# Hybrid mixer and expert layer on one core: weight casts and differences chained in the order of use, and none of the differences on POOL

## The chip, the cores and the metric

The kernel runs on one core of a Trainium2 chip. The core has five engines with queues of their own: PE (TensorE, matrix products), DVE (VectorE), ACT (ScalarE), POOL (GpSimd) and SP (SyncE, which here only issues loads). The metric is the device time of one execution in microseconds. The figure of the kernel before is the median of three runs.

## What is computed

One layer over 2048 tokens of width 1024. A layer norm comes first, then a mixer (a gated short convolution and a pooling branch between two projections) with a residual and a second layer norm. The second half is what the change touches: a hierarchical mixture of experts, a gated embedding of p beside it, and the last layer norm.

```python
mix = _hybrid_mixer(x, w_in[i], b_in[i], conv_w[i], pool_w[i], pool_scale[i], w_o[i])
x = _layernorm(DEEPNORM_ALPHA * x + mix, ln1_g[i], ln1_b[i])
ffn = _hierarchical_moe(x, w_router_group[i], b_router_group[i], w_router_expert[i],
                        b_router_expert[i], w1[i], w3[i], w2[i])
ple = jax.nn.sigmoid(x @ w_ple_gate[i] + b_ple_gate[i]) * (p[i] @ w_ple_proj[i])
x = _layernorm(DEEPNORM_ALPHA * x + ffn + ple, ln2_g[i], ln2_b[i])
```

Each token goes to one group of experts and there to two experts, `silu(x @ w1) * (x @ w3) @ w2`. Everything is float32.

## The kernel before

**Products.** A float32 product is made of three matmuls of parts: `mm3` (L222 to L224) multiplies high by high, high by low and low by high. Each operand is split first. `split` (L355 to L357) makes the high part with a cast on ACT (L356) and the low part with a difference on DVE (L357), or on the engine given to it.

**Weights.** The second half uses 414 weight tiles of 128 x 1024 in a fixed sequence. A name such as P0.8 is the weight of kind P, round 0, index 8. Kind P are the ten tiles of the embedding's gate (0 to 3 and 5 to 8) and projection (4 and 9); kinds A and B are the experts'. Rounds P0 and P1 come first, then the experts, then P99 at the end. `load_weights` issues a load on SP (L1132) into a raw slot (RB or RY), `split_weights` (L1137) takes raw tiles in the sequence of use, claims two slots of FB for the parts, issues the cast and the difference, and frees the raw slot. A slot of FB comes free when PE has used its weight. Index 4 and 9 are halved on the way (L1147 on ACT, L1148 on DVE). Of P0 and P1 the odd indexes 1, 3, 5 and 7 have their difference on POOL, eight in all.

**The embedding.** `embed` works on a group of token tiles (10 and 11 with P0, 12 to 15 with P1), the first half of the columns with weights 0 to 4 and the second with 5 to 9. For each tile four gate weights give a PSUM bank; L1280 on DVE adds the bias and frees the bank, L1286 multiplies by the product of p with the projection, L1290 adds the tile's residual, and a store L1321 on POOL writes the finished tile to `based` and frees its raw slot. The tiles of p come in pairs: `fetch_p` (L1188) loads a pair on SP into a raw slot, and `load_p` transposes it on PE (L1221, four transposes) and splits it. L1193 on SP loads the tokens themselves.

**Order.** The instructions are written by jobs that take turns. A scheduler then places them on each engine by a model of times, within the data dependences. An engine works its queue in that order: an instruction that waits holds up all behind it. PE does the router's products (L883, L884), the embedding of P0 and P1, the routing's sums (L1006 to L1026, L1094) and then, behind the barrier of a loop for overflow blocks that here runs no turn (L1707), the experts (first products L1574). Where the loop begins, the engines wait for what was issued before it, stores too.

Of the kernel before, what the change touches and what calls it, by code (L numbers as in the profile page):

```python
# [13 lines left out]
OP = mybir.AluOpType  # L14
# [60 lines left out]
PRE, END = ([10, 11], [12, 13, 14, 15]), [0, 1, 2, 3, 4, 5, 6, 7, 8, 9]  # L75
# [108 lines left out]
def hybrid_conv_pool_hmoe_encoder(ctx, tc, x, p, ln0_g, ln0_b, w_in, b_in, conv_w, pool_w, pool_scale,  # L184
                                  w_o, ln1_g, ln1_b, w_rg, b_rg, w_re, b_re, w1, w3, w2, w_pg, b_pg,
                                  w_pp, ln2_g, ln2_b, out):
    nc = tc.nc
# [3 lines left out]
    FB, RB = Parts(), Parts()  # L191
# [54 lines left out]
    for g in range(4):  # L246
        w = 2 << g
        l, r = w // 2, w // 2 - 1
# [104 lines left out]
        nc.vector.scalar_tensor_tensor(v, v, rstd[:, s:s + 1], b, op0=OP.mult, op1=OP.add)  # L353

    def split(hi, lo, src, eng=nc.vector):  # L355
        nc.scalar.copy(hi, src)  # L356
        eng.tensor_sub(lo, src, hi)  # L357

    def transpose8(src):
        b = SP.get(2, 2)  # L360
# [179 lines left out]
    def load_w(s, j):  # L540

        for i in range(4):
            if (s, j, i) in wz:
                continue
            if (s, j, i) not in raw:
                yield from wait(SR)
                fetch_w(s, j, i)
                yield
            yield from wait(SF)
            hi = SF.get()  # L550
            yield from wait(SF)
            lo = SF.get()
            r = raw.pop((s, j, i))
            split(FB[:, hi], FB[:, lo], RB[:, r])
            SR.free(r)
            wz[s, j, i] = (hi, lo)
            yield
# [128 lines left out]
    def load_wo():  # L686
# [13 lines left out]
        for g in range(4):  # L700
            c = slice(g * 128, (g + 1) * 128)
            nc.scalar.activation(RB[:, r, c], PS[:, b, c], AF.Copy, scale=colsT[:, 28 + g:29 + g])
        SP.free(b)
        split(FB[:, ph, :512], FB[:, pl, :512], RB[:, r, :512])
        SR.free(r)
        yield
# [211 lines left out]
    before = RB[:, L, 896:960].bitcast(BF)  # L918
# [216 lines left out]
                yield  # L1135

    def split_weights():  # L1137
        while True:
            while not raws:
                yield  # L1140
            while sum(i < SF.limit for i in SF.age) < 2 + claims[0]:
                yield
            kind, r, i, q = raws.popleft()
            hi, lo = SF.get(), SF.get()
            if kind == "P" and i % 5 == 4:

                nc.scalar.mul(FB[:, hi], RB[:, q], 0.5)  # L1147
                nc.vector.scalar_tensor_tensor(FB[:, lo], RB[:, q], 0.5, FB[:, hi], op0=OP.mult, op1=OP.subtract)  # L1148
            else:
                split(FB[:, hi], FB[:, lo], RB[:, q], nc.gpsimd if kind == "P" and r < len(PRE) and i % 2 else nc.vector)  # L1150
            SR.free(q)
            wt[kind, r, i] = (hi, lo)
            yield
# [180 lines left out]
    for ts in groups:  # L1334
# [9 lines left out]
        c, q = divmod(ts[-1], 4)  # L1344
# [362 lines left out]
    with tc.For_i(0, nov_n, 1) as it:  # L1707
# [6 lines left out]
        for q in range(2 * NT):  # L1714
            i, t = divmod(q, NT)
# [76 lines left out]
    def pin(ins):  # L1792

        if pinned:
            tc.add_manual_dep(ins.ins, pinned[-1].ins.name,
                              mybir.DependencyInfo(mybir.DependencyClass.NoSync, mybir.DependencyReason.DATA),
                              reason="in order")
        pinned.append(ins)
# [144 lines left out]
    order = [f for fs in plans[:-1] for f in fs] + [END[-1]] + plans[-1]  # L1943
# [40 lines left out]
```

## Time and profile before

| what | value |
|---|---|
| median of three runs | 1607.77 us (1607.4 to 1608.76) |
| the profiled execution | 1608.11 us |
| its span, first to last instruction | 1606.5 us |
| PE busy | 1549.6 us (96%) |
| DVE busy | 1169.4 us (73%) |
| ACT busy | 761.2 us (47%) |
| POOL busy | 456.0 us (28%) |
| mean granted clock of PE | 0.989 |

Durations in the prediction come from the profiled execution, whose time includes 1.6 us around the span. A timeline row gives an instruction's start, its length and, in brackets, how long its engine had stood idle before it and what ended that. Lengths of neighbours overlap by a little, since an engine begins one instruction before the last has drained.

### The profile page before, as it was taken

Reading aid. Unit: us, or ns where it says so; the run is one execution under the profiler, and the core shown is the slowest. Engines: PE = TensorE matmul, PEld = TensorE weight load, DVE = VectorE, ACT = ScalarE, POOL = GpSimd, SP = SyncE. Lnnn points to the kernel's source line nnn. Section 1 sums busy time; section 2 is a strip of 40 time slices with the busy share of each in tenths; the row PEclk is TensorE's granted clock in tenths of the full one; section 3 lists DMA queues with packets and bytes.
Section 4 is the critical chain, followed back from the end, with each engine's and each line's share of the span. In section 5 each row is a group of like instructions: output and inputs, shape, how many; then the busy total and the mean of one; then the engine's idle time right before and its main releaser. Section 6 shows DMA issues by size and latency. Waiting matters only on the chain.

```text
span 1606.5 us, 22561 instructions
## 1 busy us (share of the span) xinstructions
PE 1549.6 (96%) x7836; PEld 1308.6 (81%) x7837; DVE 1169.4 (73%) x1533; ACT 761.2 (47%) x1005; POOL 456.0 (28%) x629
## 2 busy tenths in 40 slices
PE   7999999999999998989999999999999999999893
PEld 7888878887888887778898998888888788878673
DVE  8968574245566768768878888888878876757986
ACT  6242332113111124047777777777777766652220
POOL 3537762441223225010313122111111111013521
PEclk9999999999999999999999999999999999999997
DMA  7546268986376537369698988999999887988961
GB/s 232 194 151 199 68 207 300 352 301 176 117 257 205 175 120 269 117 228 401 247 396 320 406 328 327 395 351 337 353 356 347 318 301 287 371 324 274 339 222 53
DMA packets 205613, 430.64 MB, mean 268 GB/s; under 512 B 19128, under 2 KB 70888, under 8 KB 205496
## 3 DMA queue, kind: packets, MB, share of 16 engines
q1 hardware_dynamic: 161952, 292.06, 50.8%
q0 software_dynamic: 35024, 125.65, 21.5%
q10 hardware_dynamic: 8520, 11.45, 2.0%
q8 instruction: 63, 1.03, 0.3%
q14 instruction: 54, 0.44, 0.1%
HBM read 331.95 MB, written 97.16 MB: 267 GB/s over the span
## 4 chain that ended last, share of the span: by engine, by line
PE 51%; DVE 2%; DMA 1%; issue 0%; ACT 0%; SPq 0%; POOLq 0%; POOL 0%; DVEq 0%; ACTq 0%
PE PS L222 12%; PE PS L224 12%; PE PS L223 12%; PE PS L1574 10%; PE PS L363 2%; PE PS L1520 1%; PE PS L1521 1%; PE PS L1644 1%; DMA RY<-in_p_dram 1%; DMA FB<-x1Td 0%; PE PS L1438 0%; DVE RB L1825 0%; DVE RY L1849 0%; DMA based<-RY 0%; PE PS L1221 0%
## 5 line engine op out<-in xcount | busy, mean ns | idle before, releaser
L223 PE MATMUL PS<-FB 128*128 128x512 f32 (+1 forms) x1364 | 526.0, 386 | 5.9 <-DVE FB L357 5.2
L222 PE MATMUL PS<-FB 128*128 128x512 f32 (+1 forms) x1284 | 496.5, 389 | 17.4 <-DVE ZB L1862 10.1
L224 PE MATMUL PS<-FB 128*128 128x512 f32 (+1 forms) x1284 | 493.6, 386 | 1.6 <-DMA FB<-x1Td 1.1
L357 DVE TENSOR_TENSOR FB<-RY,FB 128x1024 fp32r<-128x1024 f32 x243 | 292.3, 1228 | 51.6 <-ACT FB L356 35.1
L223 PEld LDWEIGHTS PS<-FB 128*128 128x128 f32 x1364 | 258.2, 189 | 56.1 <-DVE FB L357 6.2
L222 PEld LDWEIGHTS PS<-FB 128*128 128x128 f32 x1284 | 242.7, 189 | 66.2 <-DVE ZB L1862 10.3
L224 PEld LDWEIGHTS PS<-FB 128*128 128x128 f32 x1284 | 242.6, 189 | 50.8 <-DMA FB<-x1Td 1.6
L356 ACT CAST FB<-RY 128x1024 fp32r<-128x1024 f32 x247 | 252.6, 1051 | 55.7 <-PE PS L223 18.9
L357 DVE TENSOR_TENSOR FB<-RB,FB 128x1024 fp32r<-128x1024 f32 x197 | 238.5, 1226 | 48.4 <-ACT FB L356 35.1
L356 ACT CAST FB<-RB 128x1024 fp32r<-128x1024 f32 x201 | 207.4, 1052 | 119.6 <-PE PS L223 54.0
L1574 PE MATMUL PS<-FB 128*128 128x296 f32 (+15 forms) x1280 | 174.7, 296 | 3.9 <-issue 3.1
L1574 PEld LDWEIGHTS PS<-FB 128*128 128x128 f32 x1280 | 170.6, 191 | 5.3 <-issue 3.3
L356 ACT CAST FB<-PS 128x1024 fp32r<-128x1024 f32 (+9 forms) x142 | 81.7, 591 | 141.7 <-PE PS L363 83.3
L357 DVE TENSOR_TENSOR FB<-PS,FB 128x1024 fp32r<-128x1024 f32 (+9 forms) x142 | 96.0, 690 | 70.0 <-ACT FB L356 69.6
L1387 POOL DMA_INDIRECT RY<-x1d,TBI x22 | 56.9, 2587 | 172.4 <-DVE FB L357 115.4
L223 PE MATMUL PS<-FB,FY 128*128 128x512 f32 x264 | 104.1, 394 | 0.0
L222 PE MATMUL PS<-FB,FY 128*128 128x512 f32 x216 | 85.7, 397 | 0.0
L224 PE MATMUL PS<-FB,FY 128*128 128x512 f32 x216 | 85.4, 395 | 0.0
L356 ACT CAST FY<-RB 128x1024 fp32r<-128x1024 f32 (+1 forms) x30 | 31.0, 1035 | 109.0 <-PE PS L223 59.5
L1687 POOL DMA_DIRECT2D yd<-RY x25 | 14.3, 573 | 228.5 <-ACT RY L1686 215.6
L1387 POOL DMA_INDIRECT RB<-x1d,TBI x18 | 37.3, 2073 | 144.8 <-DVE FB L357 74.9
L222 PE MATMUL PS<-FY,FB 128*128 128x512 f32 x180 | 71.6, 398 | 0.0
(293 smaller groups left out, 2061.0 us busy)
## 6 DMA issues: line engine op xcount, KB each, us to landing
RY<-in_w_dram SPq DMA_DIRECT2D x233, 512.0 KB, 8.6
RB<-in_w_dram SPq DMA_DIRECT2D x151, 512.0 KB, 9.0
yd<-RB POOLq DMA_DIRECT2D x67, 512.0 KB, 8.0
RB<-in_w_in_dram SPq DMA_DIRECT2D x32, 512.0 KB, 5.7
yd<-RY POOLq DMA_DIRECT2D x25, 512.0 KB, 7.3
RB<-in_x_dram SPq DMA_DIRECT2D x24, 512.0 KB, 4.3
x1Td<-FB POOLq DMA_DIRECT2D x20, 512.0 KB, 6.0
FB<-x1Td SPq DMA_DIRECT2D x20, 512.0 KB, 6.4
```

The costliest lines, as they stand in the source:

```text
L222: nc.tensor.matmul(o, ah, bh, start=start, stop=False)
L223: nc.tensor.matmul(o, ah, bl, start=False, stop=False)
L224: nc.tensor.matmul(o, al, bh, start=False, stop=stop)
L356: nc.scalar.copy(hi, src)
L357: eng.tensor_sub(lo, src, hi)
L363: nc.tensor.transpose(v[:, k], src[:, k * 128:(k + 1) * 128], ident)
L1387: nc.gpsimd.indirect_dma_start(out=RB[0:half or 128, rows[n]], out_offset=None, in_=x1d, in_offset=bass.IndirectOffsetOnAxis(ap=idx, axis=0))
L1520: nc.tensor.matmul(o, xs[0][:, c], wh, start=start, stop=False)
L1521: nc.tensor.matmul(o, xs[0][:, c], wl, start=False, stop=stop)
L1574: nc.tensor.matmul(o, u, v, start=k == 0 and q == 0, stop=k == KD - 1 and q == 1)
L1644: nc.tensor.transpose(v[:, k], g[:, k * 128:(k + 1) * 128], ident[0:m, 0:m])
L1687: nc.gpsimd.dma_start(dst(n), RB[:, q])
```

## The change

`split` returns its two instructions. `split_weights` hands each weight's cast and difference to `pin`, which adds an order-only dependence on the previous one of the same engine in the same block of code. So ACT casts the weights in the sequence of use, and DVE makes the differences in it. The chain starts anew behind the loop. The eight differences that went to POOL go to DVE.

```diff
--- before.py
+++ after.py
@@ -353,8 +353,7 @@
         nc.vector.scalar_tensor_tensor(v, v, rstd[:, s:s + 1], b, op0=OP.mult, op1=OP.add)
 
     def split(hi, lo, src, eng=nc.vector):
-        nc.scalar.copy(hi, src)
-        eng.tensor_sub(lo, src, hi)
+        return nc.scalar.copy(hi, src), eng.tensor_sub(lo, src, hi)
 
     def transpose8(src):
         b = SP.get(2, 2)
@@ -1135,6 +1134,18 @@
                 yield
 
     def split_weights():
+
+        before = {}
+
+        def pin(*made):
+            for made_now in made:
+                ins = made_now.ins
+                if ins.engine in before and before[ins.engine][0] is nc.cur_bb:
+                    tc.add_manual_dep(ins, before[ins.engine][1].name,
+                                      mybir.DependencyInfo(mybir.DependencyClass.NoSync, mybir.DependencyReason.DATA),
+                                      reason="in order")
+                before[ins.engine] = nc.cur_bb, ins
+
         while True:
             while not raws:
                 yield
@@ -1144,10 +1155,10 @@
             hi, lo = SF.get(), SF.get()
             if kind == "P" and i % 5 == 4:
 
-                nc.scalar.mul(FB[:, hi], RB[:, q], 0.5)
-                nc.vector.scalar_tensor_tensor(FB[:, lo], RB[:, q], 0.5, FB[:, hi], op0=OP.mult, op1=OP.subtract)
+                pin(nc.scalar.mul(FB[:, hi], RB[:, q], 0.5),
+                    nc.vector.scalar_tensor_tensor(FB[:, lo], RB[:, q], 0.5, FB[:, hi], op0=OP.mult, op1=OP.subtract))
             else:
-                split(FB[:, hi], FB[:, lo], RB[:, q], nc.gpsimd if kind == "P" and r < len(PRE) and i % 2 else nc.vector)
+                pin(*split(FB[:, hi], FB[:, lo], RB[:, q]))
             SR.free(q)
             wt[kind, r, i] = (hi, lo)
             yield
```

The scheduler then places everything anew. In the kernel before, the casts and differences stood out of sequence in some twenty places on ACT and as many on DVE, most of them around P0, P1 and the first expert; now in none. Lines up to about L1130 have moved by -1 and lines behind by +11: L357 is now L356, L1148 is L1159, L1188 is L1199, L1221 is L1232, L1280 is L1291, L1286 is L1297, L1290 is L1301, L1321 is L1332.

DVE, from the difference of P0.8 on. Before, P0.8 (the first row), P0.9 (L1148), P1.2 and, behind the small routing steps, P1.4 (L1148):

```order
L357 TENSOR_TENSOR FB<-RY,FB 128x1024
L891 TENSOR_TENSOR ZB<-ZB,PS 36x512
L1148 SCALAR_TENSOR_TENSOR FB<-RY,FB 128x1024
L1280 TENSOR_TENSOR ZB<-PS,RB 128x512
L357 TENSOR_TENSOR FB<-RY,FB 128x1024
L1280 TENSOR_TENSOR ZB<-PS,RB 128x512
L967 TENSOR_REDUCE RB<-RB 128x4
L1286 SCALAR_TENSOR_TENSOR ZB<-ZB,PS 128x512
L968 TENSOR_TENSOR RB<-RB 128x16
L945 TENSOR_TENSOR RB<-RB 128x16
L1290 SCALAR_TENSOR_TENSOR RY<-RY,ZB 128x512
L946 TENSOR_TENSOR RB<-RB,down 128x16
```

Now, from the third row behind P0.8, which L1159 of P0.9 precedes as before: P1.0, P1.1, P1.2, P1.3 and P1.4 (L1159), with the first L1301 behind them:

```order
L356 TENSOR_TENSOR FB<-RY,FB 128x1024
L1291 TENSOR_TENSOR ZB<-PS,RB 128x512
L356 TENSOR_TENSOR FB<-RY,FB 128x1024
L1291 TENSOR_TENSOR ZB<-PS,RB 128x512
L356 TENSOR_TENSOR FB<-RY,FB 128x1024
L966 TENSOR_REDUCE RB<-RB 128x4
L1297 SCALAR_TENSOR_TENSOR ZB<-ZB,PS 128x512
L356 TENSOR_TENSOR FB<-RY,FB 128x1024
L1159 SCALAR_TENSOR_TENSOR FB<-RY,FB 128x1024
L967 TENSOR_TENSOR RB<-RB 128x16
L944 TENSOR_TENSOR RB<-RB 128x16
L1301 SCALAR_TENSOR_TENSOR RY<-RY,ZB 128x512
```

The differences of P1.0 and of P1.6, which stood ahead of P0.8, and those of P1.1 and P1.3, which POOL made, have moved in between.

PE, at the transposes of the RY tile of p. Before, they stood behind the routing sums of L1026:

```order
L1026 LDWEIGHTS RB
L1026 MATMUL PS<-OH,RB 128x32
L1221 MATMUL PS<-ident,RB 128x128 x4
L1221 MATMUL PS<-ident,RY 128x128 x4
L1019 LDWEIGHTS RB
L1019 MATMUL PS<-ZB,RB 128x64
L222 MATMUL PS<-FB 128x512
```

Now they stand ahead of P1.5, which is tile 12's second half, behind its last matmul with P1.3:

```order
L222 MATMUL PS<-FB 128x512
L223 MATMUL PS<-FB 128x512
L224 MATMUL PS<-FB 128x512
L1232 MATMUL PS<-ident,RY 128x128 x4
L222 MATMUL PS<-FB 128x512
```

The transposes of the RB tile follow 24 rows later, with the L1006 of the routing.

SP, at the loads of p. Before:

```order
L1193 DMA RY<-x1d 128x1024 x3
L1188 DMA RB<-in_p_dram 128x2x256
L1188 DMA RY<-in_p_dram 128x2x256
L1193 DMA RY<-x1d 128x1024
L1130 TENSOR_LOAD EOR
```

Now:

```order
L1204 DMA RY<-x1d 128x1024 x3
L1199 DMA RY<-in_p_dram 128x2x256
L1199 DMA RB<-in_p_dram 128x2x256
L1204 DMA RY<-x1d 128x1024
L1129 TENSOR_LOAD EOR
```

The two loads of p have changed places.

At the loop, POOL issues three of the last four stores ahead of it instead of four and the fourth behind it, one L1290 of DVE stands behind it too, and the first sixteen L1574 of PE, which stood ahead of the loop, now stand behind it with the rest.

## Rows read from the trace of the kernel before

**Rows 1.** Page, part 1: busy time, share of span, instructions of each engine.
```profile
PE 1549.6 (96%) x7836; PEld 1308.6 (81%) x7837; DVE 1169.4 (73%) x1533; ACT 761.2 (47%) x1005; POOL 456.0 (28%) x629
```

**Rows 2.** Busy time by stretch: stretch, length, five engines, PEclk, DMA share, GB/s.
```profile
645.20:648.60 3.40, 3.40 (x10) 2.63 (x9) 0.87 (x7) 0.00 (x0) 0.00 (x0) 0.50 0.66 242
1527.60:1532.60 5.00, 5.00 (x14) 4.12 (x15) 3.20 (x5) 1.69 (x3) 2.21 (x3) 0.50 0.93 342
```

**Rows 3.** Waits of PE, 590 to 760: engine line, releaser, total, times, longest.
```profile
PE PS L1574 <- issue: 3.1, 1, 3.1
PE PS L223 <- DVE FB L357: 2.9, 1, 2.9
PE PS L222 <- DVE ZB L1280: 2.9, 1, 2.9
PE PS L222 <- DVE FB L357: 1.3, 1, 1.3
```

**Rows 4.** Timeline of PE, 625 to 655: start, length, instruction, [idle before, releaser].
```profile
626.40 0.39 PE L884 MATMUL PS<-FB 128*128 128x512 f32 x1
629.73 0.50 PE L223 MATMUL PS<-FB 128*128 128x512 f32 x1 [2.94 <-DVE FB L357]
...
640.67 0.39 PE L224 MATMUL PS<-FB 128*128 128x512 f32 x1
643.94 0.50 PE L222 MATMUL PS<-FB 128*128 128x512 f32 x1 [2.88 <-DVE ZB L1280]
...
652.23 0.60 PE L1221 MATMUL PS<-ident,RY 128*128 128x128 f32 x4
```

**Rows 5.** Timeline of DVE, 624 to 650.
```profile
626.60 3.07 DVE L357 TENSOR_TENSOR FB<-RY,FB 128x1024 fp32r<-128x1024 f32 x1 [0.23 <-PE PS L883]
...
632.33 1.23 DVE L357 TENSOR_TENSOR FB<-RY,FB 128x1024 fp32r<-128x1024 f32 x1
633.48 0.68 DVE L1280 TENSOR_TENSOR ZB<-PS,RB 128x512 f32<-128x512 f32 x1
...
635.86 2.90 DVE L1290 SCALAR_TENSOR_TENSOR RY<-RY,ZB 128x512 f32<-128x512 f32 x1
...
640.66 0.68 DVE L1290 SCALAR_TENSOR_TENSOR RY<-RY,ZB 128x512 f32<-128x512 f32 x1
...
643.21 0.68 DVE L1280 TENSOR_TENSOR ZB<-PS,RB 128x512 f32<-128x512 f32 x1
```

**Rows 6.** Timeline of POOL, 610 to 720.
```profile
625.25 3.34 POOL L357 TENSOR_TENSOR FB<-RY,FB 128x1024 fp32r<-128x1024 f32 x1
...
635.77 2.45 POOL L357 TENSOR_TENSOR FB<-RY,FB 128x1024 fp32r<-128x1024 f32 x1
639.06 0.57 POOL L1321 DMA_DIRECT2D based<-RY  x1 [0.85 <-DVE RB L946]
...
709.73 0.53 POOL L1321 DMA_DIRECT2D based<-RY  x1 [0.84 <-DVE RY L1290]
```

**Rows 7.** Timeline of SP, 630 to 660: issues of loads.
```profile
641.94 0.38 SPq L1188 DMA_DIRECT2D RB<-in_p_dram  x1
643.99 0.38 SPq L1188 DMA_DIRECT2D RY<-in_p_dram  x1
```

**Rows 8.** DMA issues, whole run: times, KB each, median us from issue to landing.
```profile
RY<-in_p_dram SPq DMA_DIRECT2D x5, 256.0 KB, 6.1
...
RB<-in_p_dram SPq DMA_DIRECT2D x3, 256.0 KB, 3.9
```

**Rows 9.** Timeline of PE, 1522 to 1537.
```profile
1527.54 1.08 PE L1221 MATMUL PS<-ident,RY 128*128 128x128 f32 x4 [4.76 <-DMA RY<-in_p_dram]
```

**Rows 10.** Chain that ended last, 700 to 725.
```profile
712.30 3.33 DMA based<-RY
715.63 1.33 issue
```

**Rows 11.** Timeline of PE, 704 to 730.
```profile
711.33 2.55 PE L1574 MATMUL PS<-FB 128*128 128x384 f32 x16 [0.78 <-DVE ZB L1286]
```

## The prediction

> **What bounds the kernel now.** I read the page's busy times first: PE works 1549.6 of the 1606.5 us [rows 1], so a weight's cast or difference counts only where PE stands waiting for it. The waits of PE around the first two weight rounds come next [rows 3]. There are four that matter: 2.9 us for a low part on DVE, 2.9 us for L1280 on DVE, 1.3 us for another low part and 3.1 us before the first matmuls behind the loop. They are what this change can win between 590 and 760 us, where nearly all the moved instructions are. Last come the timelines of the engines in that stretch.
>
> The first wait is at 629.73: PE's last router matmul starts at 626.40 and the next weight, P0.8, is missing its low part [rows 4]. Its slot is freed by that router work, DVE starts the difference at 626.60 and needs 3.07 us, where the same form takes 1.23 us at 632.33 [rows 5]; POOL's own difference runs from 625.25 for 3.34 us beside it [rows 6]. The second is at 643.94: PE's last matmul before it starts at 640.67, lasts 0.39 us, and tile 12's second half needs the bank that L1280 frees [rows 4], which DVE reaches only at 643.21 [rows 5]. Here, too, POOL held DVE up: L1290, half as wide as a weight, takes 2.90 us at 635.86 [rows 5] beside POOL's difference from 635.77 for 2.45 us [rows 6].
>
> **Part 1: eight differences leave POOL for DVE.** A moved one costs DVE about 1.15 us, the step from 632.33 to 633.48 when it runs back to back [rows 5]. What DVE gets back is the contention: 3.07 - 1.23 = 1.84 us at 626.60 and 2.90 - 0.68 = 2.22 us at 635.86, taking 0.68 us, the length of L1280 at 633.48, as what a 512-wide operation takes [rows 5]. Six of the moved or delayed differences fall between 627 and 645 us and cost 6 x 1.15 = 6.9 us against 4.1 us won, so DVE is later by 2.8 us at the end of the stretch, less what it idled. The first wait shrinks for certain: with POOL silent, the low part of P0.8 takes 1.23 us from 626.60, and PE restarts at 627.9 instead of 629.73, 1.85 us earlier.
>
> The Trainium skill (SBUF — State Buffer, section "Who interferes with whom") says that a DVE instruction with two SBUF inputs and a GpSimd instruction that reads SBUF shut each other out for the whole instruction. By that rule DVE would lose all of POOL's time, the move would be a gain on DVE, and the sum would be that of the faster rival below. The trace shows such blocks in two rows and elsewhere DVE idling while POOL works, so I keep the 4.1 us.
>
> **Part 2: the chain moves DVE's queue.** After P0.8's low part DVE now does, in this order: L891, the low parts of P0.9 and P1.0, L1280, P1.1, L1280, P1.2, L1286, P1.3, P1.4, L1290 and three small steps. That is 6 x 1.15 + 5 x 0.68 + some 0.3 = 10.6 us, so L1290 ends at 627.8 + 10.6 = 638.4. Before, it ended at 635.86 + 2.90 = 638.76 [rows 5]: the added work and the removed contention nearly cancel here. Behind it stand three more low parts (3.45), one L1286 and one L1290 (1.36), the small steps that took 1.9 us from the end of L1290 at 641.34 to 643.21 [rows 5], and L1280 itself (0.68); so L1280 of tile 12 ends at about 645.8 instead of 643.89.
>
> **Part 3: PE's order puts four transposes of p in front of that wait.** This decides my forecast. In the changed order the L1221 transposes of the RY tile of p stand ahead of P1.5, where PE waited at 643.94. Before, they ran at 652.23 [rows 4], long after their data. Their load is bound to a chain: L1290 ends, POOL stores the finished tile (issue 639.06 [rows 6], 0.3 us after L1290), the store lands and frees the slot, and SP issues the load in the same moment, at 643.99 [rows 7]; that is 4.93 us from store to load. SP has the two loads of p swapped, so the RB one (641.94, [rows 7]) no longer goes first, which does not bring the RY one forward: it waits for the store, and the RB one now waits behind it. Now: L1290 638.4, store 638.7, load 643.6. A load of p takes 3.9 us (median of three into RB) to 6.1 us (median of five into RY) from issue to landing [rows 8]. I take 3.8, near the shorter, since this stretch has little other traffic and the longer median holds loads from the crowded end; the bounds are 3.3, which a store twice its size took behind 712.30 [rows 10], and 6.1. PE is ready at 641.06 - 1.85 = 639.2 and stands until 647.4: 8.2 us instead of 2.88. P1.5 starts after the transposes (0.5 us) at 647.9, 4.0 us later than before, and the transposes are missing later on, so the net is **+3.5 us** (bounds +3.0 and +5.8). L1280, done at 645.8, is hidden behind it.
>
> That such a wait happens in this kernel is seen near the end: the same L1221 stood 4.76 us for the same load at 1527.54 [rows 9].
>
> **Part 4: the clock.** After the wait at 643.94 the granted clock was half for the 3.4 us from 645.2, after the longer one at 1527.54 for 5.0 us [rows 2]. Half the clock for a stretch loses half of it: 1.7 us before. After an 8.2 us wait I take the longer stretch, 2.5 us: **+0.8** (0 to +1.7, the latter for twice the shorter stretch). The Trainium skill (TensorE: Matmul & The Clock Gate, section "What's actually happening") has the clock fall to half when the array idles and return after sustained work; the trace agrees with 0.50 behind both waits, and by that rule too a longer wait costs more than its own length.
>
> **Part 5: the loop.** Ahead of the loop POOL now makes three of the four stores of the last tiles instead of four; the fourth, and the sixteen L1574 matmuls that PE did at 711.33 in 2.55 us [rows 11], stand behind it. Before, the last store was issued at 712.30, landed 3.33 us later and PE went on 1.33 us after that [rows 10]. The third was issued at 709.73, 2.6 us earlier [rows 6]. So PE could go on up to 2.6 us earlier, but carries 2.55 us more work behind the loop: between 0 and +2.55. I take 1.0 of the 2.6, since the last products of P1.9 now run in one group: **+1.6**.
>
> **Part 6: the rest.** Of the 414 weights only some twenty changed places on each engine, most of them here. Further on their casts wait for slots that PE frees, and PE does not wait for them: 0 (-1 to +1). With PE held to 647, DVE gets ahead, so the wait of 1.3 us for a low part [rows 3] should halve: **-0.7** (-1.3 to 0). The casts on ACT change places only.
>
> **Sum.** +3.5 + 0.8 + 1.6 - 0.7 = +5.2 us. The first wait's 1.85 us are in the 3.5. The profiled run took 1608.11 us (its span 1606.5 and 1.6 around it), 0.34 above the median of the three runs, so 1613.3 on its scale and **1613.0 us** on the median's. A measurement of this kernel tells about 0.2% (3.2 us) from no change: faster is under 1604.6, slower over 1611.0.
>
> **Rivals.**
> 1. *PE does not wait for p* (no change). If the load is in by 645.3, L1280 decides: P1.5 at 645.8, +1.9; with +1.6 at the loop and -0.7 this gives +2.8, or 1610.6. For it: the load's two medians lie 2.2 us apart. Against: store and load together took 4.9 and at least 3.3 us, so they end at 646.9 from 638.7.
> 2. *POOL's block was the whole cost* (faster). If DVE wins more than 4.1 us from a silent POOL, L1290 and its store come earlier by as much, and the waits at 629.73 and 643.94 and the half clock go: -1.85 - 2.9 - 1.7 + 1.6 = -4.9, or 1602.9. It decides only if both L1280 and p are there by 639.2, 6.6 us and 8.2 us sooner than worked out. For it speaks that POOL held up both of the instructions that PE waited for or stood behind; against it, that DVE has six more weights to do in that time.
> 3. *The fourth store starves the weights* (much slower). It holds a raw slot across the loop, and SP loads in order: the load into that slot waits for it, and those behind too. Issue behind the loop plus a landing of 3.3 us [rows 10] puts some loads 4 us later, +9 in all, 1617. Against: the weights behind have casts much later.
> 4. *The chain does nothing that PE feels*: 1607.8.
>
> **How the numbers follow.** Forecast 0.43, rival 1 0.25, rival 2 0.12, rival 3 0.10, rival 4 0.10. Slower: 0.43 + 0.10 = 0.53; same: 0.35; faster: 0.12. The range from 1606.0 to 1617.0 takes in rivals 1 and 4 and the bounds of part 3, and leaves out rival 2 and half of rival 3.
>
> **What would show it.** PE's wait for a low part at 629.7 down to about 1 us; a wait of L1221 for RY<-in_p of 6 to 9 us near 640; half clock behind it for 3 to 5 us; no L357 on POOL; 96 matmuls of L1574 in one run behind the loop. I am wrong if L1221 finds its data there, if PE's idle time between 620 and 660 falls below 5.8 us, or if a new wait comes up among the experts, where PE is busy throughout.

## Result and profile after: slower, by more than the range allowed

The changed kernel takes 1620.2 us (median of four runs, 1616.87 to 1622.95), the kernel before 1607.68 beside it (1607.4 to 1608.76): 1.0072 times as long, 95% interval 1.0057 to 1.0088. Run once more beside other kernels (e12 below) it stood at 1.0053 (1.0034 to 1.0073). The sign was forecast; the predicted 1613.0 was 7 us short, and the range ended at 1617.0.

The profiled execution of after took 1622.95 us, its span 1621.3. Part 1 of its page answers [rows 1]:

```profile
PE 1559.7 (96%) x7837; PEld 1319.3 (81%) x7837; DVE 1171.3 (72%) x1541; ACT 759.6 (47%) x1005; POOL 442.6 (27%) x621
```

POOL has given up 13.4 us, DVE has only 1.9 more, and PE is *busy* 10.1 us longer on the same matmuls. The same work at a lower clock takes longer, and PE's mean granted clock is 0.979 here, where it was 0.989 before. The waits of PE between 590 and 760 us answer [rows 3] (engine, line, releaser: total, times, longest):

```profile
PE PS L1232 <- issue: 8.0, 1, 8.0
PE PS L1585 <- issue: 6.5, 1, 6.5
PE PS L1585 <- ACT ZB L1293: 1.2, 1, 1.2
PE PS L223 <- DVE FB L356: 1.1, 1, 1.1
PE PS L222 <- DVE ZB L1036: 0.8, 1, 0.8
```

The wait for L1280 (now L1291) is gone; the transposes of p wait instead, and the loop's wait has doubled. The timelines of after answer [rows 4 to 7] (start, length, instruction, idle before it):

```profile
629.33 0.50 PE L223 MATMUL PS<-FB 128*128 128x512 f32 x1 [1.09 <-DVE FB L356]
640.01 0.53 POOL L1332 DMA_DIRECT2D based<-RY  x1 [28.67 <-DVE RY L1301]
645.45 0.68 DVE L1291 TENSOR_TENSOR ZB<-PS,RB 128x512 f32<-128x512 f32 x1
645.86 0.38 SPq L1199 DMA_DIRECT2D RY<-in_p_dram  x1
648.63 1.09 PE L1232 MATMUL PS<-ident,RY 128*128 128x128 f32 x4 [7.95 <-issue]
...
688.70 10.73 PE L1093 MATMUL PS<-RB,RY 128*128 128x40 f32 x64
699.92 0.80 PE L222 MATMUL PS<-FB 128*128 128x512 f32 x1 [0.49 <-DVE TBH L1099]
...
708.15 1.07 PE L222 MATMUL PS<-FB 128*128 128x512 f32 x4
...
732.17 5.05 PE L1585 MATMUL PS<-FB 128*128 128x384 f32 x20 [6.51 <-issue]
```

This execution was 1.45 us later than before's already at the router, from half clock in the first 40 us; the next execution of the same program (e12) was 0.24 us later there. The chain of work that ended last, at the loop, answers [rows 10]:

```profile
726.03 4.62 DMA based<-RY
730.66 1.51 issue
732.17 7.90 PE PS L1585 x40
```

The prediction does not speak of L1093, the small matmuls of 40 columns that put the token numbers into blocks by masks which DVE makes (L1088). They are 32 instructions of the program and 64 in the trace. Before they ran in two halves of 32:

```profile
674.01 3.66 PE L1094 MATMUL PS<-RB,RY 128*128 128x40 f32 x32
677.50 0.47 PE L222 MATMUL PS<-FB 128*128 128x512 f32 x1
...
681.72 3.66 PE L1094 MATMUL PS<-RB,RY 128*128 128x40 f32 x32
...
694.86 1.07 PE L222 MATMUL PS<-FB 128*128 128x512 f32 x4
```

A half took 3.49 us to the next matmul's start, with 18 products of 0.227 us between the halves. In after all 64 stand in one run and take 10.73 us instead of twice 3.49. The windows of after through that run say why (stretch, length, PE, PEld, DVE, ACT, POOL, PEclk, DMA share, GB/s):

```profile
690.00:691.00 1.00, 1.00 (x12) 1.00 (x11) 0.39 (x1) 0.00 (x0) 0.00 (x0) 1.00 0.00 0
692.00:693.00 1.00, 1.00 (x7) 1.00 (x7) 0.36 (x1) 0.00 (x0) 0.00 (x0) 0.50 0.00 0
696.00:697.00 1.00, 1.00 (x7) 1.00 (x6) 0.00 (x0) 0.00 (x0) 0.00 (x0) 0.50 0.00 0
704.00:705.00 1.00, 1.00 (x4) 0.82 (x3) 0.99 (x1) 0.00 (x0) 0.08 (x1) 0.50 1.06 410
706.00:707.00 1.00, 1.00 (x6) 0.80 (x5) 0.41 (x1) 0.56 (x1) 0.00 (x0) 1.00 1.02 410
```

PE is busy for the whole of each of these microseconds, and yet its clock falls to 0.50 (1.2 instead of 2.4 GHz) near 692 and is back only near 705.6, among the products behind. Before, the clock was 1.00 through the same work, from the first small matmul to the first product of P1.8 (window of before):

```profile
674.00:694.80 20.80, 20.80 (x125) 18.39 (x124) 10.65 (x14) 6.46 (x7) 2.94 (x3) 1.00 0.55 198
```

### The profile page after: what moved, and what is told of

Same layout as the page of the kernel before. It is cut to its first block, busy times and chain, and to the rows that moved or that the text cites. A ratio compares the mean times of both kernels' runs of the same rounds, so it can differ in the third digit from the quotient of the medians.

```text
span 1621.3 us, 22544 instructions
## 1 busy us (share of the span) xinstructions
PE 1559.7 (96%) x7837; PEld 1319.3 (81%) x7837; DVE 1171.3 (72%) x1541; ACT 759.6 (47%) x1005; POOL 442.6 (27%) x621
## 4 chain that ended last, share of the span: by engine, by line
PE 89%; DVE 5%; issue 2%; POOL 2%; DMA 1%; ACT 1%; POOLq 0%; DVEq 0%; ACTq 0%
PE PS L222 23%; PE PS L224 23%; PE PS L223 23%; PE PS L1585 10%; PE PS L362 3%; PE PS L1531 1%; PE PS L1532 1%; DVE FB L356 1%; PE PS L1093 1%; PE PS L1655 1%; DVE RY L1836 1%; DVE RB L1836 0%; DVE RY L1860 0%; PE PS L882 0%; PE PS L883 0%
## 5 line engine op out<-in xcount | busy, mean ns | idle before, releaser
L356 DVE TENSOR_TENSOR FB<-RY,FB 128x1024 fp32r<-128x1024 f32 x247 | 294.6, 1218 | 53.5 <-ACT FB L356 35.2
L356 ACT CAST FB<-RY 128x1024 fp32r<-128x1024 f32 x247 | 251.7, 1051 | 61.3 <-PE PS L224 27.9
L356 DVE TENSOR_TENSOR FB<-RB,FB 128x1024 fp32r<-128x1024 f32 x201 | 242.8, 1224 | 49.7 <-ACT FB L356 38.9
L356 ACT CAST FB<-RB 128x1024 fp32r<-128x1024 f32 x201 | 206.8, 1050 | 108.6 <-PE PS L223 50.4
L1585 PE MATMUL PS<-FB 128*128 128x296 f32 (+15 forms) x1280 | 175.5, 297 | 8.3 <-issue 6.5
L1585 PEld LDWEIGHTS PS<-FB 128*128 128x128 f32 x1280 | 171.1, 191 | 10.0 <-issue 6.9
L356 ACT CAST FB<-PS 128x1024 fp32r<-128x1024 f32 (+9 forms) x142 | 82.1, 591 | 152.8 <-PE PS L362 92.7
L356 DVE TENSOR_TENSOR FB<-PS,FB 128x1024 fp32r<-128x1024 f32 (+9 forms) x142 | 96.1, 689 | 64.6 <-ACT FB L356 64.2
L1398 POOL DMA_INDIRECT RY<-x1d,TBI x22 | 61.6, 2800 | 178.1 <-DVE FB L356 131.7
L356 ACT CAST FY<-RB 128x1024 fp32r<-128x1024 f32 (+1 forms) x30 | 31.0, 1034 | 111.1 <-PE PS L223 59.6
L348 POOL TENSOR_SCALAR rstd<-mv 128x1 f32<-128x1 f32 x41 | 34.1, 831 | 144.8 <-DVE mv L343 118.7
```

Source lines behind the costliest of these rows:

```text
L348: nc.gpsimd.tensor_scalar(rstd[:, s:s + 1], mv[:, s, 1:2], EPS, None, op0=OP.add)
L356: return nc.scalar.copy(hi, src), eng.tensor_sub(lo, src, hi)
L1398: nc.gpsimd.indirect_dma_start(out=RB[0:half or 128, rows[n]], out_offset=None, in_=x1d, in_offset=bass.IndirectOffsetOnAxis(ap=idx, axis=0))
L1585: nc.tensor.matmul(o, u, v, start=k == 0 and q == 0, stop=k == KD - 1 and q == 1)
```

## The experiments

Nearly all the kernels below write PE's order down: the instructions of the block ahead of the loop are collected, and a list of numbers chains them by order-only dependences. Only 430 instructions, from the first that moved, are in the list. The lists are written here as OLD (before's order) and NEW (after's), m is the place of the first L1093 in NEW, and a second list, where there is one, is for DVE. The lines of these kernels have moved by +30 to +32, those of e3 and e4 not at all. Ratios are to the kernel before on the same chip, which stood at 1608.8 to 1609.3 us in those sessions.

**e1: all of the change, but PE's order of before.** Theory A: what is lost is lost by PE's order. Theory B: by the work on DVE and ACT.

```diff
     nc = tc.nc
+    entry = nc.cur_bb.bb
...
+    made = {ins.name: ins for ins in entry.instructions}
+    for numbers in PLACED:
+        chain = [made[f"I-{n}"] for n in numbers]
+        for a, b in zip(chain, chain[1:]):
+            tc.add_manual_dep(b, a.name,
+                              mybir.DependencyInfo(mybir.DependencyClass.NoSync, mybir.DependencyReason.DATA),
+                              reason="in order")
...
+PLACED = [OLD]
```

> The changed kernel in full (chains on ACT and DVE, all differences on DVE), but the 430 matmuls and transposes of PE from the first one that the change moved to the loop are held in the order of the kernel before. Theory A, PE's order is the whole loss (the transposes ahead of P1.5, the 64 matmuls of the masks in one block, the loop): 1605 to 1611 us, no wait of PE for the transposes of p, no half clock around 690 to 705. Theory B, six more differences make DVE the bound in this stretch: 1614 to 1620 us, with PE waiting for DVE around 640 to 700.

1607.47 us, 0.9995 (0.9985 to 1.0005): theory A. The casts, differences and POOL's release cost nothing that these runs can tell, as long as PE keeps its order. The wait for P0.8 is 1.09 us, but the next one has grown from 2.88 us [rows 3] (timeline of PE):

```profile
645.12 0.77 PE L252 MATMUL PS<-FB 128*128 128x512 f32 x1 [5.62 <-DVE ZB L1321]
```

L1321 is the old L1280: DVE reaches it later by what it took over from POOL.

**e2: the kernel before with PE's order of after.**

```diff
+PLACED = [NEW]
```

> The kernel before (no chains, eight differences on POOL), with the same 430 instructions of PE held in the order of the changed kernel. Theory A: 1616 to 1623 us, with a wait of 6 to 9 us at the transposes of p and half clock behind the block of 64 mask matmuls. Theory B: 1607 to 1611 us, since DVE has no more to do than before.

1616.13 us, 1.0047 (1.0028 to 1.0066). The order alone costs 7 us without any of the edits. The p transposes stand 8.34 us, and the small matmuls end at half clock:

```profile
651.39 1.09 PE L1251 MATMUL PS<-ident,RY 128*128 128x128 f32 x4 [8.34 <-issue]
...
691.01 3.66 PE L1124 MATMUL PS<-RB,RY 128*128 128x40 f32 x32
695.11 5.09 PE L1124 MATMUL PS<-RB,RY 128*128 128x40 f32 x32 [0.43 <-DVE RY L1119]
```

**e3: only the eight differences moved to DVE, no chain, the scheduler's own order.**

```diff
-                split(FB[:, hi], FB[:, lo], RB[:, q], nc.gpsimd if kind == "P" and r < len(PRE) and i % 2 else nc.vector)
+                split(FB[:, hi], FB[:, lo], RB[:, q])
```

> Only the second part of the change: the eight differences go from POOL to DVE, no chains; the scheduler is free. Its PE order has the eight transposes of p behind tile 12's second half, as before, but the 64 mask matmuls in one block, as in the changed kernel. Theory A: no wait at the transposes, 1611 to 1616 us, the loss all at the block and at the loop, with half clock behind the block. Theory B: 1614 to 1620 us with waits for DVE. If the block costs nothing: 1605 to 1609 us.

1614.29 us, 1.0033 (1.0022 to 1.0043), as theory A had it. There is no wait for p, but the L1093 matmuls stand in one run, with half clock from 686 to 697 us.

**e4: only the chain, POOL keeps its differences.**

```diff
-                pin(*split(FB[:, hi], FB[:, lo], RB[:, q]))
+                pin(*split(FB[:, hi], FB[:, lo], RB[:, q], nc.gpsimd if kind == "P" and r < len(PRE) and i % 2 else nc.vector))
```

> Only the first part of the change: casts and differences are chained on each engine, POOL keeps its eight differences (in a chain of its own). Its PE order has four of the transposes five matmuls earlier than before and the mask matmuls in two blocks. Theory A: 1605 to 1611 us, as before within 0.2%. A theory C, that holding the sequence of use itself delays weights: 1613 us or more, with waits of PE for L357.

1613.01 us, 1.0024 (1.0014 to 1.0035): 2 us above theory A's range and just at the edge of theory C's, but without the waits for L357 that theory C named. The chain puts POOL's differences of P1 into 632 to 647 us, side by side with DVE's urgent work, and PE waits 7.74 us for tile 12's bank. What POOL does to DVE (timeline of both):

```profile
635.64 2.62 POOL L356 TENSOR_TENSOR FB<-RY,FB 128x1024 fp32r<-128x1024 f32 x1 [0.73 <-ACT ZB L1293]
...
636.59 1.71 DVE L967 TENSOR_TENSOR RB<-RB 128x16 f32<-128x16 f32 x1
638.22 0.16 DVE L944 TENSOR_TENSOR RB<-RB 128x16 f32<-128x16 f32 x1
```

Two operations of the same size: 1.71 us beside POOL's difference, until it ends at 638.26, and 0.16 us behind it. The Trainium skill (SBUF — State Buffer, section "Who interferes with whom") says that a DVE instruction with two SBUF inputs contends with a GpSimd instruction that reads SBUF, and calls the port pair that they share an exclusive lock. This row agrees: the DVE operation ended at 638.30, right behind POOL's difference.

**e5 and e6: the list cut in two.** e5 has before's order up to the end of P1.4 and after's behind it, e6 the reverse.

```diff
-PLACED = [OLD]
+PLACED = [OLD[:208] + [n for n in NEW if n not in OLD[:208]]]
```

> The changed kernel with PE's order of before up to the last product of P1.4 (so the transposes of p stand behind the routing sums again), and behind that PE's order of the changed kernel, with the 64 mask matmuls in one block. If the places add up: the wait for p goes, but PE then waits 5 to 6 us for the bank that L1280 frees, as in the run with the old PE order, so only 2 to 5 us are won: 1614 to 1618 us, and the half clock behind the mask block stays. If the wait for p were most of the loss: 1607 to 1611 us.

```diff
-PLACED = [OLD]
+PLACED = [[n for n in NEW if n in OLD[:208]] + [n for n in OLD if n not in OLD[:208]]]
```

> The reverse: PE's order of the changed kernel up to there (transposes of p ahead of P1.5), behind that the order of before, with the mask matmuls in two blocks and 18 matmuls of 512 columns between them. If the mask block and what follows it are more than half of the loss: 1609 to 1614 us with a wait of 6 to 9 us for p and no half clock between 690 and 705. If the wait for p were most of it: 1616 to 1620 us.

1614.68 us, 1.0028 (1.0012 to 1.0044), and 1615.31 us, 1.0035 (1.0023 to 1.0048). Either half of the list loses by itself, and the two losses add up to about that of the change. e6, whose only long wait is that for p (7.98 us), lies between its two forecasts, 1 us above the nearer one; e5, whose only new trait is behind P1.4, shows that a second loss of the same size lies there.

**e7: after with 18 products moved between two halves of the small matmuls.**

```diff
-PLACED = [NEW]
+PLACED = [NEW[:m - 18] + NEW[m:m + 16] + NEW[m - 18:m] + NEW[m + 16:]]
```

> The changed kernel with one edit in PE's order: the 18 matmuls ahead of the 64 mask matmuls move between their halves. If the block itself costs, by its waits for the masks (10.7 against 7.3 us) and by the clock (half for some 12 us behind it, which loses 6): 3 to 9 us less than the changed kernel, 1611 to 1617 us. If only the sum of the mask matmuls counts, wherever they stand: 1618 to 1622 us.

1620.63 us, 1.0065 (1.0045 to 1.0085): no gain. The products came from ahead of the masks, so PE reached the first half 3.39 us ahead of DVE's first mask, and the clock fell behind that wait:

```profile
687.19 7.05 PE L1123 MATMUL PS<-RB,RY 128*128 128x40 f32 x32 [3.39 <-DVE RY L1118]
...
699.74 3.66 PE L1123 MATMUL PS<-RB,RY 128*128 128x40 f32 x32
```

**e8: e1, with the bank's release ahead of three other steps on DVE.** L1280 of tile 12 (4751) goes ahead of an L1286 and of the differences of P1.6 and P1.7.

```diff
-PLACED = [OLD]
+PLACED = [OLD, [4645, 4751, 4620, 4675, 4702, 4621]]
```

> The changed kernel with the old PE order, and on DVE L1280 of tile 12, which frees the PSUM bank that PE waits for at 645, ahead of L1286 and the differences of P1.6 and P1.7 instead of behind them. In the run with the old PE order PE waited 5.6 us there and ran at half clock for 6 us after. If that wait is DVE's queue alone, it falls to 1 to 2 us and the half clock goes: 1599 to 1604 us, faster than both kernels. If the wait only moves to the next weights: 1606 to 1609 us.

1608.17 us, 0.9995 (0.9983 to 1.0006): the wait only moved. It fell from 5.62 to 2.19 us, and 1.80 us for the routing's one-hot rows came up behind it, with half clock around the masks.

**e9: e7, with DVE making the first two masks ahead of an L1291, both L1297 and three L1301.**

```diff
-PLACED = [NEW]
+PLACED = [NEW[:m - 18] + NEW[m:m + 16] + NEW[m - 18:m] + NEW[m + 16:],
+          [4512, 4763, 4513, 4514, 4515, 4521, 4523, 4516, 4522, 4525, 4542, 4773, 4771, 4781, 4772, 4782, 4558, 4576]]
```

> The changed kernel with the 64 matmuls of the masks cut in halves, 18 products from ahead of them now between the halves, and on DVE the first two masks put ahead of the second L1291, both L1297 and three L1301, so that PE does not wait for them (in the run with the halves alone PE waited 3.39 us there). Theory C: the late loss is the clock, which fell behind 64 small matmuls in one run (0.50 from 693.5 to 705.2 us, 11.7 us, so 5.8 us lost). Then there is no half clock between the halves and behind them, and the time is 1611 to 1615 us: 1620.6 of the run with halves less 3.4 and less 3 to 5. Theory D: the late loss lies elsewhere (the loop, masks that wait for slots): 1617 to 1621 us.

1612.53 us, 1.0014 (1.0002 to 1.0027): the time that theory C named, but not all of it for theory C's reason. The wait at the masks is gone. The clock still fell behind either half, without a wait ahead of the first (timeline, then windows):

```profile
685.00 3.90 PE L1125 MATMUL PS<-RB,RY 128*128 128x40 f32 x32
...
694.38 3.66 PE L1125 MATMUL PS<-RB,RY 128*128 128x40 f32 x32
```

```profile
688.70:691.70 3.00, 3.00 (x8) 2.42 (x9) 2.84 (x3) 0.00 (x0) 0.00 (x0) 0.50 0.12 27
698.50:702.00 3.50, 3.47 (x9) 2.73 (x10) 0.00 (x0) 0.61 (x1) 2.27 (x3) 0.53 0.83 270
```

From the first mask to P1.8 it loses 4.2 us against full clock, no less than the 3.8 of e12 beside it. What it gained lies at the loop, where the scheduler now hides sixteen matmuls ahead of it: from P1.8 to the 129th of the first expert's matmuls it takes 60.5 us, e12 66.0.

**e10: e1 with one thing of the new order, the small matmuls in one run.**

```diff
-PLACED = [OLD]
+PLACED = [OLD[:290] + OLD[308:324] + OLD[290:308] + OLD[324:]]
```

> The changed kernel with PE's order of before (1607.5 us) and one thing of the new order: the 64 matmuls of the masks in one run, the 18 products that stood between their halves behind them. Theory C (a run of 64 small matmuls lets the clock fall, which costs about 6 us): half clock from the middle of the run on for 8 to 12 us, and 1611 to 1614 us. Theory D: no half clock beyond 3 us, 1606 to 1609 us.

1614.45 us, 1.0032 (1.002 to 1.0044), where e1 had 0.9995: some 6 us for moving 18 products from between the halves to behind them. No other order on PE was touched. The two ratios are of two sessions, so by their intervals the price is about 3 to 9 us. The two profiled executions are 8.8 us apart: 3.2 us between the first small matmul and P1.8 (5.0 us lost against full clock, e1 1.8), 1.3 us from there to the first expert's 129th matmul, and the rest where nothing was moved. Timeline, and a window that begins inside the run:

```profile
676.87 9.47 PE L1123 MATMUL PS<-RB,RY 128*128 128x40 f32 x64
```

```profile
681.50:691.50 10.00, 10.00 (x37) 8.84 (x37) 1.81 (x4) 0.00 (x0) 2.97 (x3) 0.50 0.88 307
```

Ten microseconds, all busy, all at half clock. This is theory C at its plainest.

**e11: after with its own PE order, DVE making the first two masks earlier.**

```diff
-PLACED = [NEW]
+PLACED = [NEW, [4512, 4763, 4513, 4773, 4514, 4515, 4521, 4523, 4516, 4522, 4525, 4542, 4771, 4781, 4772, 4782, 4558, 4576]]
```

> The changed kernel with its own PE order, but on DVE the first two masks ahead of both L1297 and three L1301; with that the scheduler puts the sixteen matmuls of the first expert back ahead of the loop. The masks' matmuls stay in one run of 64. Theory E: the loop costs about 4.4 us in the changed kernel (6.51 us of standing, then sixteen matmuls at half clock, 10.8 us from the last product of P1.9 to the 21st of L1585's matmuls against 6.4 before): 1615 to 1617 us. Theory C alone (the run of 64 matmuls is all of the late loss): 1618.5 to 1621 us.

1624.61 us, 1.0093 (1.0075 to 1.011): slower than after and than either theory had it, so it prices nothing. The two L1297 that gave way free a bank, and PE now waits there, with half clock behind it:

```profile
687.31 0.80 PE L254 MATMUL PS<-FB 128*128 128x512 f32 x1 [3.83 <-DVE ZB L1329]
```

**e12: the changed kernel again**, the same program with its order as a list.

```diff
+PLACED = [NEW]
```

> The changed kernel once more, word for word the same program, with its PE order written down as a list. It is there to be compared with the three others on the same chip: 1620 us, 1617 to 1623 as its four runs spread. Theory E wants the run with the masks first at least 3 us below it, theory C the one with the fed halves at least 6 us below it.

1617.5 us (1616.03 to 1622.43), 1.0053. Of the same 64 matmuls:

```profile
687.24 8.11 PE L1123 MATMUL PS<-RB,RY 128*128 128x40 f32 x64
```

Here the clock fell near 693.4, 6 us behind the first of the 64, where it fell 3.3 us behind it in the profile above, and was back near 700.2. So one program takes 8.11 us for the run here and 10.73 there, and by that alone its times differ by microseconds.

**e13: e9, but the 18 products spread among the 64 small matmuls.**

```diff
-PLACED = [NEW[:m - 18] + NEW[m:m + 16] + NEW[m - 18:m] + NEW[m + 16:],
+mix, g = [], NEW[m - 18:m]
+for k in range(32):
+    mix.append(NEW[m + k])
+    if (k % 2 == 1 or k in (0, 30)) and g:
+        mix.append(g.pop(0))
+PLACED = [NEW[:m - 18] + mix + NEW[m + 32:],
```

> The changed kernel with the fed masks of e9_masks_fed, but the 18 products spread among the 64 matmuls of the masks, one behind every three or four of them, where e9 had them all between the halves. In e9 the clock still fell behind either half (0.50 from 688.7 to 691.5 and from 698.7 to 702 us), with PE busy throughout. Theory C2 (the small matmuls in a row let the clock fall, not a wait): the clock stays at 1.00 from the first mask to P1.8, the stretch loses under 1 us where e9 lost 4.2, and the time is 2 to 5 us below e9, 1607.5 to 1610.5. Theory D2 (it is the masks' form itself or a wait that the rows do not show): half clock in the stretch as before, and 1611 to 1614 us.

1622.23 us, 1.0085 (1.0068 to 1.0102): 10 us above e9, the opposite of what I expected. The clock fell behind a wait for a bank and did not come back until products ran alone again (timeline, then windows):

```profile
687.47 0.50 PE L254 MATMUL PS<-FB 128*128 128x512 f32 x1 [2.70 <-DVE ZB L1329]
```

```profile
688.50:708.00 19.50, 19.50 (x76) 17.64 (x76) 2.94 (x5) 0.00 (x0) 0.00 (x0) 0.50 0.31 101
708.00:712.20 4.20, 4.20 (x11) 3.37 (x11) 0.16 (x1) 1.05 (x1) 2.96 (x3) 0.50 1.06 409
```

Whether the mixture would also have let the clock fall without the 2.70 us stays open. That it does not let it rise is shown: 19.5 us of the mixture at 0.50, and 1.00 again only among the products behind it.

**e14: after with the p transposes moved behind the first 18 products of P1.5.**

```diff
-PLACED = [NEW]
+PLACED = [NEW[:136] + NEW[140:158] + NEW[136:140] + NEW[158:]]
```

> The changed kernel with its own PE order, but the four transposes of the RY tile of p moved behind the first 18 products of P1.5, which they stood ahead of; with that the scheduler also puts the sixteen matmuls back ahead of the loop. Theory P (prediction's part 3 and its first rival: without the wait for p, L1291 of tile 12 decides): no wait of L1232 over 1 us, a wait of 5.3 to 6.0 us for L1291 in its place, so 2.5 us less there, and with the loop's 2 to 5 us the time is 1610 to 1614 us where the changed kernel took 1617.5 on the same kind of count. If the wait only moves on behind the transposes (theory M), a wait of 2 us or more comes up behind P1.5 and the time is 1614 to 1618 us.

1615.59 us, 1.0042 (1.0027 to 1.0057). L1232 finds its data, and L1291 of tile 12 is next, as the prediction's first rival had it; but another wait follows, so it is theory M's time:

```profile
646.25 0.77 PE L252 MATMUL PS<-FB 128*128 128x512 f32 x1 [5.62 <-DVE ZB L1321]
...
654.55 0.50 PE L252 MATMUL PS<-FB 128*128 128x512 f32 x1 [1.40 <-DVE FB L386]
```

**e15: the edits of e13 and e14 together.**

```diff
-PLACED = [NEW[:m - 18] + mix + NEW[m + 32:],
+x = NEW[:m - 18] + mix + NEW[m + 32:]
+PLACED = [x[:136] + x[140:158] + x[136:140] + x[158:],
```

> Both edits of e13_masks_mixed and e14_p_later in the changed kernel. If the two places and the loop are all that the change loses, it stands at the kernel before less the 1.85 us of the first wait, plus the 2.7 us by which the wait for L1291 is longer than before: within 2 us of the kernel before, 1606.5 to 1610.5 us. If something else is lost behind them, 1611 us or more.

1625.25 us, 1.0103 (1.0084 to 1.0122), for the reason of e13: half clock from 686 to 709 us.

**e16, e17, e18: before, with one or two differences off POOL, PE's order of before, no chain.** POOL's rows at 625.25 and 635.77 [rows 6] are P1.1 and P1.3. e16 moves the first, e17 the second, e18 both. The line of e18 (the others name one pair):

```diff
-                split(FB[:, hi], FB[:, lo], RB[:, q], nc.gpsimd if kind == "P" and r < len(PRE) and i % 2 else nc.vector)
+                split(FB[:, hi], FB[:, lo], RB[:, q], nc.gpsimd if kind == "P" and r < len(PRE) and i % 2 and (r, i) not in ((1, 1), (1, 3)) else nc.vector)
...
+PLACED = [OLD]
```

> The kernel before with its own PE order, where only the difference of P1.1 leaves POOL for DVE, no chain. It is the one that ran on POOL from 625.25 for 3.34 us beside P0.8's low part. By the contention rule of part 1 P0.8's wait falls from 2.94 to 1.09 us and DVE is 0.7 us ahead behind it (1.84 won, 1.15 spent), so of the 1.85 us that PE comes earlier some 0.7 us are left at the wait for L1280: 1606.5 to 1608.5 us if the kernel before stands at 1608.8. Rival 2 of the prediction (POOL's block is the whole cost of such waits): 1605 to 1606.5 us.

> The same with only the difference of P1.3, which ran on POOL from 635.77 for 2.45 us beside L1290. By the rule of part 1 DVE comes 1.1 us earlier to tile 12's L1280 (2.22 won, 1.15 spent), the wait there falls from 2.88 to about 1.8 us with a little less half clock: 1607 to 1608.5 us if the kernel before stands at 1608.8. If DVE is no earlier, 1608.5 to 1610.

> Both, P1.1 and P1.3, on DVE, P1.5, P1.7 and P0's four still on POOL, PE order of before. By the rule of part 1: the wait of P0.8 is 1.09 us, that for L1280 about 3 us, 1606 to 1607.5 us if the kernel before stands at 1608.8. Rival 2: both waits near 1 us and no half clock, 1603 to 1605 us.

1606.13 us, 0.9984 (0.9975 to 0.9994); 1605.52 us, 0.9976 (0.9966 to 0.9986); 1602.85 us, 0.9959 (0.9946 to 0.9973). Before stood at 1609.34 us here, 0.5 us above what the expectations took. With that taken off, e16 falls in rival 2's range, and e17 lies 2 us below its own. e18 beats both kernels, and by more than either account had: part 1's rule wanted waits of 1.09 and about 3 us, rival 2 both near 1 us. They are 2.03 and 1.06 us (PE, then DVE and POOL of e18):

```profile
629.68 0.50 PE L253 MATMUL PS<-FB 128*128 128x512 f32 x1 [2.03 <-DVE FB L387]
642.08 0.50 PE L252 MATMUL PS<-FB 128*128 128x512 f32 x1 [1.06 <-DVE ZB L1310]
```

```profile
627.28 2.35 DVE L387 TENSOR_TENSOR FB<-RY,FB 128x1024 fp32r<-128x1024 f32 x2
...
632.39 3.39 POOL L387 TENSOR_TENSOR FB<-RB,FB 128x1024 fp32r<-128x1024 f32 x1 [6.11 <-PE PS L254]
...
635.82 0.68 DVE L1320 SCALAR_TENSOR_TENSOR RY<-RY,ZB 128x512 f32<-128x512 f32 x1
```

P1.1's difference now runs ahead of P0.8's on DVE (the two at 627.28), so that wait shrinks by 0.9 us instead of 1.85; L1320, the old L1290, is back at 0.68 from 2.90 us. The half clock behind 643.94 [rows 2] is gone too. In the profile that is 0.9 + 1.8 + 1.7 = 4.4 us by P1.8, where e18, counted from the router on, is 4.3 us earlier than before; the other 2.4 us of that execution come mostly from a shorter wait for p near the end [rows 9], 2.62 us for 4.76, where nothing was changed. Nor is it shown that the shorter wait for the bank saved the 1.7 us of half clock: e16 stood 2.88 us there, as before did, and kept 1.00 behind it (timeline, then window):

```profile
643.46 0.50 PE L252 MATMUL PS<-FB 128*128 128x512 f32 x1 [2.88 <-DVE ZB L1310]
```

```profile
644.40:648.00 3.60, 3.60 (x21) 2.71 (x20) 1.21 (x10) 0.07 (x1) 0.00 (x0) 1.00 0.79 296
```

## Why the prediction was wrong

The trace gives the loss by stretch. From the first small matmul to P1.8 lie 64 small matmuls (2 x 3.49 us) and 60 products before or 24 after (0.227 us each): 20.6 and 12.4 us at full clock. They took 20.85 us before, 19.45 in after, 16.20 in e12.

| us more than before, in profiled executions | predicted | after | e12 |
|---|---|---|---|
| up to the router | 0 | +1.45 | +0.24 |
| router to the small matmuls (parts 1 to 4) | +4.3 | +5.07 | +4.82 |
| small matmuls to P1.8 | 0 | +6.77 | +3.52 |
| P1.8 to the 129th matmul of the first expert (part 5, low part of 6) | +0.9 | +3.29 | +2.31 |
| behind it | 0 | -1.73 | -0.18 |
| sum | +5.2 | +14.85 | +10.71 |

The second line is what is left of P1.8's delay (13.3 us in after, 8.6 in e12) when the first and the third are taken off. The last stretch took 846.2 us in after and 847.8 in e12, the same program, so a difference of one or two microseconds between two profiled executions tells nothing.

- **Parts 1 to 3, the wait for p: right.** On before's scale (1.45 us taken off) the store is issued at 638.6 (predicted 638.7), the load at 644.4 (643.6), the transposes start at 647.2 (647.4), P1.5 at 647.9 (647.9). The wait is 7.95 us (8.2). That it comes out so closely is in part luck: from store to load it took 5.9 us (4.9 worked out), from load to transposes 2.8 (3.8, and 3.3 as the lower bound), and the two misses cancel. In e12 they are 5.1 and 3.8 us. P0.8's wait shrank by 1.85 us, as worked out. L1291 ended at 644.7 (645.8), hidden behind the wait. e14 shows what the first rival's L1291 is worth without that wait: 5.6 us, and then 1.4 more, so little is won.
- **Part 4, the clock behind that wait: nearly right.** 0.50 from 648.6 to 654.4 us, 2.9 us lost, 1.2 more than before; predicted 0.8. A wait of 0.8 us for L1036 came on top, of which the prediction has nothing. With these the second line is accounted for: -1.85 at P0.8, 7.95 instead of 2.88 us at the next wait, 1.2 for the clock and 0.8 for L1036 make +5.2, and +5.07 was measured.
- **Part 6, "0 (-1 to +1)" for the rest of the order: the step that failed.** I asked of each moved instruction whether PE would wait for it. The L1093 matmuls had moved together into one run; PE does not wait for them, and at this step the prediction has no line for what they do to the clock. The runs show +6.8 us there in after and +3.5 in e12. e10 shows the price with everything else as in e1: about 6 us by the medians, and in this stretch of the traces 3.2 us. Over all kernels, the loss against full clock between the first small matmul and P1.8, waits of up to 0.9 us included, was 3.8 to 7.0 us in the eight with one run (after, e2, e3, e5, e10, e11, e12, e14), and with 14 to 18 products between two halves and no wait ahead 0.2 to 0.3 us (before, e4, e17, e18), some 1.8 (e1, e8, e16) or, in e9, 4.2. With a wait ahead of the halves it was 1.9 (e6) and 7.4 (e7). These are one trace each, and the same program lost 7.0 us in after and 3.8 in e12. So the run is what costs, and halves are safer but not safe; why the clock held between the halves of before and not between those of e9 stays open.
- **The low part of part 6, -0.7: not seen.** Before, that wait stood at 708.89, behind P1.8. It is gone, but L1585 waits 1.17 and 0.63 us in the same stretch of after.
- **Part 5, the loop: right that it costs, wrong in what could be won.** The third store was to come 2.6 us earlier than the fourth did before. Counted from the first product of P1.8, before issued its third store at 14.9 and its fourth at 17.4 us; after issued its third at 17.9, e12 at 16.7. It also took 4.62 us to land (e12 4.41) instead of 3.33 [rows 10], so PE went on 1.9 us later (e12 0.6) where I had 1.0 earlier. The sixteen matmuls behind the loop then ran at half clock, 4.3 instead of 2.55 us, but that adds little, since before, too, the first sixteen behind the loop took 3.9. With the low part of part 6 the whole line is +2.3 to +3.3 instead of +0.9.
- **The experts: right.** No new wait comes up there: from 735 to 1440 us no wait of PE in after is longer than 0.4 us. So rival 3, whose 1617 lies nearest to the measured time, is not what happened. The other two signs of error did not come either: L1232 did wait, and PE's idle time between 620 and 660 us rose from 5.8 to 9.0.
- **Rival 2, POOL's block: dismissed too lightly.** It cannot win with eight differences moved, which e1 shows: 0.9995. But the blocks were real, two of the eight made them, and moving those two alone wins 0.41%. I had both numbers in part 1 (4.1 us won for 6.9 spent) and summed over all eight, where each should have been weighed by itself: P1.1 and P1.3 win 1.84 and 2.22 us for 1.15 each. Of P1.1's win PE saw 0.7 us (e16, a wait of 2.25 instead of 2.94 us), since its difference now runs ahead of P0.8's.

The range was too narrow because the clock had a term only behind waits that I had counted.

## What to carry to other kernels

When a change moves instructions, look not only for waits but also for what now stands side by side on TensorE: a long run of small matmuls can halve the clock while the engine shows as busy, and small ones mixed among products can keep it halved (e13). The run cost 3 to 9 us here against two halves with products between (e10 and e1), though halves did not hold the clock in every order (e9). When an engine's work is in another's way, move only the instructions that collide on the stretch that PE waits for: with PE's order of before, two differences off POOL won 6.5 us, of which 4.3 can be placed, and all eight, with the chain, won nothing. Sequence of use is not sequence of urgency: a small step that frees a bank or a slot may have to pass weights that are used earlier.

## What the hardware showed that I had not expected

- The clock falls while TensorE is busy without a gap: 0.50 from 692 to 699 us in after at a busy share of 1.00. The Trainium skill (TensorE: Matmul & The Clock Gate, section "What's actually happening") ties the clock to how busy the engine has recently been; the busy share of these rows does not show that state, so the granted clock has to be read by itself.
- Products mixed with small matmuls stayed at half clock for 19.5 us, and the clock rose only among products without them (e13).
- An operation on 16 elements per partition took 1.71 us on DVE beside a difference on POOL, and 0.16 us behind it (e4).
